# Joined attention runs, reworked reciprocal roots and a rearranged closing norm in a hybrid encoder layer

## The chip, the cores and the metric

The kernel runs on one core of one Trainium2 chip. The metric is the device time of one execution in microseconds; the median of three runs is given. The profile comes from one further execution and has its own time.

## The reference

One layer on 512 tokens of width 2048 (a grid of 8 rows by 64 columns). All arrays are float32.

```python
xn = rms_norm(x, attn_norm_g[l])
proj = jnp.einsum("bsd,dc->bsc", xn, w_in[l])
u_val, u_gate, q, k, v = jnp.split(proj, split_pts, axis=-1)      # 1024 columns each
y_conv = conformer_conv(u_val, u_gate, ...)   # GLU, depthwise conv of 31, layer norm, swish
y_na = neighborhood_attention(heads(q), heads(k), heads(v), rpb[l])   # 16 heads of 64
mixed = jnp.concatenate([rms_norm(y_conv, conv_out_g[l]), rms_norm(y_na, na_out_g[l])], axis=-1)
x = x + jnp.einsum("bsc,cd->bsd", mixed, w_out[l])
xn = rms_norm(x, ffn_norm_g[l])
up = depthwise_conv(jnp.einsum("bsd,df->bsf", xn, w_up[l]), ffn_dw_w[l], ffn_dw_b[l])   # width 3
gate, val = jnp.split(up, 2, axis=-1)                              # 5632 columns each
x = x + jnp.einsum("bsf,fd->bsd", jax.nn.silu(gate) * val, w_down[l])
return rms_norm(x, final_norm_g)
```

The attention lets each token see a window of 8 rows by 16 columns around it, with a learned bias per head and offset, softmax over the 128 positions, and a weighted sum of the values.

## The kernel before

Activations stand transposed: 128 channels on the partitions, 512 tokens along the free axis. Every large matmul is done with split operands: a float32 matrix is written as a high part (what float32r keeps) and a low part (the rest), and three float32r products stand for one float32 product. For a weight unit of 128 x 1024 `parts` (L123) makes the high half on ACT (`whi`, L126) and the low half on VectorE (`wlo`, L127).

The stages, in order of time, are:

1. Input projection, up to about 505 us. `project` (L334) makes one block of 128 columns in two units of eight channel blocks. `group` (L146) issues for each unit 16 matmuls with `whi` (L150, L151) and then eight with `wlo` (L153): 24 matmuls. `ORDER` (L59) fixes which blocks come when: an "a" is a gate and a value block of the convolution group, a "q" is the query, key and value blocks of a pair of heads.
2. Output projection (`out_half`, L566), first the convolution half, then the attention half.
3. The up projection (`up`, L706), in a seven-product (Strassen) form, 44 hidden tiles, with the depthwise convolution of width 3 behind each (`hidden`, L771; its taps on VectorE are L763 and L764).
4. The down projection (`product2`, L837), also of seven products, over the hidden tiles, most of which were written to HBM and come back through `again` (L809).
5. The closing norm (`ready`, `write`).

Small work between the large matmuls is written as generators. `tick` (L158) is called after each unit: it takes the next step of the first generator in `steps` and of the first in `asteps`, and places its instructions after the unit's last matmul. So one step stands on TensorE between two groups of 24 matmuls. Inside that, a scheduler orders each engine's instructions by priority; `shifted` (L85) moves the priority, `pin` keeps instructions in the order in which they were written.

`attend` (L450) is the generator of one pair of heads. Its steps before the change, one per tick:

- the value tile's transposes (`trv`, L458) and the load of the first bias table (L521);
- `scores(0)`: for two of the four blocks of 128 queries, both heads, a matmul of 64 rows on 256 keys (L470) into the one PSUM tile with the tag "sc"; then for each head bias (L478), maximum (L480), exponentials on ACT (L483), reciprocal (L484) and scaling on ACT (L486);
- the second table;
- `scores(2)` and the first `turn`: the transposes (`trp`, L498) of the first two blocks' weights, one PSUM tile with the tag "tr" (two buffers) per head, and ACT's copy of each (L503);
- `values(0)`: the products with the values (L512);
- the second `turn`;
- `values(2)`, the copy and the split.

The convolution taps (L384, 30 for each of eight tiles, on VectorE) run alongside at a later priority, each on the accumulator `y` of its tile.

`root_steps` (L232) makes an inverse root of 512 sums: a root on ACT, a reciprocal and one Newton step on VectorE (L237 to L241), a diagonal matrix per 128 tokens (L245), and one float32 matmul with ones (L248) that spreads the result over all partitions. It is run five times. PSUM for it comes from `stat` (L225), the "sc" tile up to the output projection, "tr" after.

`TURN2` (L55) is the order of the down projection's products. Its operands are made by `operand` (L783): a copy on ACT (L801), a subtraction on VectorE (L802). The first two (`KEEP // 2`) are made ahead, during the last hidden tile, in `again`.

In the last product (`TAIL`, L57) the four banks end one after the other. For each, `ready` (L893) adds the residual (L898) and sums squares on ACT (L900); when both banks of a token block are done `write` (L905) forms the inverse root and scales and stores the rows.

Of the kernel before, what the change touches and what calls it, by code (L numbers as in the profile page):

```python
# [10 lines left out]
F32 = mybir.dt.float32  # L11
F32R = mybir.dt.float32r
AF = mybir.ActivationFunctionType
# [3 lines left out]
P = 128  # L17
# [56 lines left out]
def layer(ctx: ExitStack, tc: tile.TileContext, xT, xn, w_in, w_out, w_up, w_down, par, tab, g3, out):  # L74
# [17 lines left out]
    def t2(name, dt=F32):  # L92
        return tp.tile([P, S], dt, tag="t2k", name=name)
# [20 lines left out]
    eps = consts.tile([P, 1], F32, name="eps")  # L114
    nc.vector.memset(eps, EPS)
    ident = consts.tile([P, P], F32, name="ident")
    make_identity(nc, ident)

# [113 lines left out]
    def root_steps(sums, n, name):  # L232

        v, r, y = (sm.tile([P, S // P], F32, tag="rs" + c, name="rs" + c) for c in "vry")
        nc.vector.tensor_scalar(v, sums, 1.0 / n, EPS, op0=ALU.mult, op1=ALU.add)
        nc.scalar.activation(r, v, AF.Sqrt)
        nc.vector.reciprocal(r, r)  # L237
        nc.vector.tensor_mul(y, v, r)
        nc.vector.tensor_mul(y, y, r)
        nc.vector.tensor_scalar(y, y, -0.5, 1.5, op0=ALU.mult, op1=ALU.add)  # L240
        nc.vector.tensor_mul(y, y, r)  # L241

        dg = t2("dg")
# [4 lines left out]
        nc.tensor.matmul(ps, ones, dg, start=True, stop=True)  # L248
        res = t2(name)
        nc.scalar.activation(res, ps, AF.Copy)  # L250
        return res
# [198 lines left out]
    def attend(p, q, k, v):  # L450


        hps = [slice(j * DH, (j + 1) * DH) for j in range(2)]
        vt = []
        for half in range(2):
            ps = psa.tile([P, 4, P], F32, tag="tr", name="trv", bufs=2)
            for c in range(4):
                nc.tensor.transpose(ps[:, c, :], v[half][:, c // 2, c % 2 * P:(c % 2 + 1) * P], ident)  # L458
            t = t2("vt").rearrange("p (c k) -> p c k", c=4)
            nc.scalar.activation(t, ps, AF.Copy)  # L460
            vt.append(t)
        po = psa.tile([P, S], F32, tag="po", name="po")
        soft = []

        def scores(b0):
            both = psa.tile([P, 2, 2, 2 * P], F32, tag="sc", name="sc")
            for i in range(2):
                b = b0 + i
                for j, hp in enumerate(hps):
                    m = nc.tensor.matmul(both[:, j, i, :], q[hp, b * P:(b + 1) * P], grid(k, KC0[b], KW)[hp],  # L470
                                         start=True, stop=True)
                    if i or j:
                        pin(m)
            two = tabs.pop(0)
            for j in range(2):
                tb = two[:, j]
                s = t2("s").rearrange("p (i k) -> p i k", i=2)
                nc.vector.scalar_tensor_tensor(s, both[:, j], DH ** -0.5, tb, op0=ALU.mult, op1=ALU.add)  # L478
                nm = sm.tile([P, 2], F32, tag="nm", name="nm")
                nc.vector.tensor_reduce(nm, s, axis=AX.X, op=ALU.max, negate=True)  # L480
                su = sm.tile([P, 2], F32, tag="su", name="su")
                for i in range(2):
                    nc.scalar.activation(s[:, i], s[:, i], AF.Exp, bias=nm[:, i:i + 1], accum_out=su[:, i:i + 1])  # L483
                nc.vector.reciprocal(su, su)  # L484
                for i in range(2):
                    nc.scalar.activation(s[:, i], s[:, i], AF.Copy, scale=su[:, i:i + 1])  # L486
                soft.append(s)

        pts = []

        def turn():
            pts.clear()
            for j in range(2):
                s = soft.pop(0)
                ps = psa.tile([P, 4, P], F32, tag="tr", name="trp", bufs=2)
                for i in range(2):
                    for ch in range(2):
                        m = nc.tensor.transpose(ps[:, 2 * i + ch, :], s[:, i, ch * P:(ch + 1) * P], ident)  # L498
                        if i or j or ch:
                            pin(m)  # L500
                pt = t2("pt").rearrange("p (c k) -> p c k", c=4)
                with shifted(-SOONER):
                    nc.scalar.activation(pt, ps, AF.Copy)  # L503
                pts.append(pt)

        def values(b0):
            for i in range(2):
                b = b0 + i
                for ch in range(2):
                    for j in (1, 0):  # L510
                        hp = hps[j]
                        m = nc.tensor.matmul(grid(po, b * BLK, BLK)[hp], vt[b // 2][:, 2 * (b % 2) + ch, hp],  # L512
                                             pts[j][:, 2 * i + ch, :], start=(ch == 0), stop=(ch == 1))
                        if (i, ch, j) != (0, 0, 1):
# [378 lines left out]
    def ready(x, ps, th, dh, only=range(2 * Q), fused=()):  # L893

        for i in only:
            t, d = divmod(i, Q)
            d += Q * dh
            add(x[i], x[i], ps[i])  # L898
            q = t2("sq")
            nc.scalar.activation(q, x[i], AF.Square, accum_out=sq[th][:, t, d:d + 1])  # L900
            if i not in fused:
                nc.vector.tensor_mul(x[i], x[i], gs[d])
            yield

    def write(th, t, ys, fused=()):  # L905
        v, r, y = (sm.tile([P, 1], F32, tag="rs" + c, name="rs" + c) for c in "vry")
        nc.vector.tensor_reduce(v, sq[th][:, t], axis=AX.X, op=ALU.add)
        nc.scalar.activation(r, v, AF.Sqrt, scale=1.0 / D, bias=eps)
        nc.vector.tensor_scalar(v, v, 1.0 / D, EPS, op0=ALU.mult, op1=ALU.add)
        nc.vector.reciprocal(r, r)  # L910
        nc.vector.scalar_tensor_tensor(y, v, r, r, op0=ALU.mult, op1=ALU.mult)
        nc.vector.tensor_scalar(y, y, -0.5, 1.5, op0=ALU.mult, op1=ALU.add)
        nc.vector.tensor_mul(y, y, r)
        for d in reversed(range(Q)):
            for dh in range(2):
                i = t * Q + d
                x = ys[dh][i]
                if dh:
                    nc.scalar.activation(x, x, AF.Copy, scale=y)
                elif i in fused:  # L920
                    nc.vector.scalar_tensor_tensor(x, x, y, gs[d], op0=ALU.mult, op1=ALU.mult)
# [35 lines left out]
    for i in product2(5, a, False):  # L957
        with shifted(-100):
            for _ in ready(e3, a, 0, 0, (i,), fused):
                pass  # L960
        if i % Q == Q - 1:
            for _ in write(0, i // Q, (e3, e0), fused):
                pass


# [60 lines left out]
```

## Time and profile before

| what | us |
|---|---|
| median of 3 runs | 1992.7 (1992.6 to 1993.33) |
| the profiled execution, its time | 1993.17 |
| its span | 1991.4 |
| TensorE busy (PE) | 1976.7 |
| VectorE busy (DVE) | 1593.1 |
| ScalarE busy (ACT) | 1100.4 |
| mean granted TensorE clock | 0.998 |

Engines are PE (matmuls), PEld (weight loads), DVE (VectorE), ACT (ScalarE), POOL (GpSimd) and SP (which issues DMAs). A line such as L470 is a line of the kernel. The page's second part divides the span into 40 slices, each digit the busy share in tenths. The chain of waits is followed back from the last instruction to what released it; its rows give start, length and what. A timeline row gives start, length, engine, line, operation, tile written and read, shape, and in brackets the engine's idle time before it and what ended it. A row of grouped instructions ends in busy time, mean duration in ns, and idle time before. A row of a window gives each engine's busy time and count in the order PE, PEld, DVE, ACT, POOL, then the granted clock, the DMA share and GB/s. Matmuls are pipelined, so the duration of one is longer than the distance to the next.

### The profile page before, as it was taken

Reading aid. Unit: us, or ns where it says so; the run is one execution under the profiler, and the core shown is the slowest. Engines: PE = TensorE matmul, PEld = TensorE weight load, DVE = VectorE, ACT = ScalarE, POOL = GpSimd, SP = SyncE. Lnnn points to the kernel's source line nnn. Section 1 sums busy time; section 2 is a strip of 40 time slices with the busy share of each in tenths; the row PEclk is TensorE's granted clock in tenths of the full one; section 3 lists DMA queues with packets and bytes.
Section 4 is the critical chain, followed back from the end, with each engine's and each line's share of the span. In section 5 each row is a group of like instructions: output and inputs, shape, how many; then the busy total and the mean of one; then the engine's idle time right before and its main releaser. Section 6 shows DMA issues by size and latency. Waiting matters only on the chain.

```text
span 1991.4 us, 28519 instructions
## 1 busy us (share of the span) xinstructions
PE 1976.7 (99%) x10525; PEld 1685.7 (85%) x10525; DVE 1593.1 (80%) x2296; ACT 1100.4 (55%) x1728; POOL 225.4 (11%) x310
## 2 busy tenths in 40 slices
PE   9999999999999999999999999999999999999998
PEld 7878888887788888989898898989898888888886
DVE  5995798498547888888888888888888898886764
ACT  7244423438525675666666666656666644554653
POOL 0111111110001111111111111111110400000000
PEclk9999999999999999999999999999999999999999
DMA  9676667666857889999999999999986967666563
GB/s 345 176 219 186 170 169 209 182 181 186 278 148 199 216 220 271 243 267 247 262 252 257 263 245 262 248 265 244 268 228 179 362 244 231 220 215 195 192 201 116
DMA packets 143117, 451.04 MB, mean 226 GB/s; under 512 B 15232, under 2 KB 23936, under 8 KB 141568
## 3 DMA queue, kind: packets, MB, share of 16 engines
q1 hardware_dynamic: 90608, 293.98, 43.2%
q0 software_dynamic: 42624, 148.92, 34.8%
q10 hardware_dynamic: 9744, 6.30, 1.0%
q8 instruction: 83, 1.36, 0.3%
q14 instruction: 58, 0.48, 0.1%
HBM read 430.27 MB, written 111.15 MB: 272 GB/s over the span
## 4 chain that ended last, share of the span: by engine, by line
PE 96%; DVE 2%; DMA 1%; ACT 0%; issue 0%; SPq 0%; DVEq 0%
PE pu L720 37%; PE pd L848 21%; PE pj L150 7%; PE pj L153 7%; PE pj L151 7%; PE po L150 3%; PE po L151 3%; PE po L153 3%; PE pu L143 2%; PE pu L142 2%; PE pu L139 2%; DVE y L384 1%; PE sc L470 1%; PE po L512 1%; PE trp L498 1%; DMA raw<-in_w_in 0%
## 5 line engine op out<-in xcount | busy, mean ns | idle before, releaser
L127 DVE TENSOR_TENSOR wlo<-raw,whi 128x1024 fp32r<-128x1024 f32 x572 | 694.6, 1222 | 285.2 <-ACT whi L126 221.4
L126 ACT ACTIVATE whi<-raw 128x1024 fp32r<-128x1024 f32 x572 | 600.7, 1058 | 572.7 <-PE pj L151 168.0
L720 PE MATMUL pu<-xc,whi 128*128 128x512 f32 x2112 | 505.5, 391 | 0.1
L720 PEld LDWEIGHTS pu<-xc,whi 128*128 128x128 f32 x2112 | 388.0, 188 | 75.3 <-DVE xc L603 0.3
L848 PE MATMUL pd<-whi,ho 128*128 128x512 f32 x1232 | 305.1, 389 | 1.4 <-DVE vl L733 1.4
L720 PEld LDWEIGHTS pu<-xc,wlo 128*128 128x128 f32 x2112 | 274.4, 191 | 10.3
L720 PE MATMUL pu<-xc,wlo 128*128 128x256 f32 x2112 | 282.3, 283 | 0.0
L848 PEld LDWEIGHTS pd<-whi,ho 128*128 128x128 f32 x1232 | 231.0, 188 | 50.3 <-DVE vl L733 1.8
L150 PE MATMUL pj<-xh,whi 128*128 128x512 f32 x608 | 241.4, 397 | 0.0
L151 PE MATMUL pj<-xl,whi 128*128 128x512 f32 x608 | 237.6, 391 | 0.0
L384 DVE SCALAR_TENSOR_TENSOR y<-ch,prm,y 128x510 f32<-128x510 f32 (+14 forms) x240 | 169.8, 739 | 3.1
L848 PE MATMUL pd<-wlo,ho 128*128 128x512 f32 x616 | 165.0, 389 | 0.0
L153 PE MATMUL pj<-xh,wlo 128*128 128x512 f32 x608 | 150.4, 389 | 0.8 <-DVE wlo L127 0.8
L729 ACT ACTIVATE pu<-pu 128x512 f32<-128x512 f32 x132 | 76.5, 580 | 121.4 <-PE pu L720 121.2
L150 PEld LDWEIGHTS pj<-xh,whi 128*128 128x128 f32 x608 | 114.2, 188 | 27.4 <-issue 4.9
L848 PEld LDWEIGHTS pd<-wlo,ho 128*128 128x128 f32 x616 | 115.6, 188 | 24.0
L153 PEld LDWEIGHTS pj<-xh,wlo 128*128 128x128 f32 x608 | 114.0, 188 | 24.9 <-DVE wlo L127 1.2
L151 PEld LDWEIGHTS pj<-xl,whi 128*128 128x128 f32 x608 | 114.2, 188 | 23.5 <-issue 1.1
L205 POOL DMA_DIRECT2D ws<-in_w_down x88 | 79.5, 904 | 363.8 <-DMA ws<-in_w_down 132.9
L664 POOL DMA_DIRECT2D raw<-in_w_up x88 | 78.0, 887 | 286.3 <-DVE wlo L127 114.5
L139 PE MATMUL pu<-xc,whi 128*128 128x256 f32 x352 | 99.6, 283 | 0.0
L142 PE MATMUL pu<-xc,whi 128*128 128x256 f32 x352 | 99.6, 283 | 0.0
(189 smaller groups left out, 2322.9 us busy)
## 6 DMA issues: line engine op xcount, KB each, us to landing
raw<-in_w_up SPq DMA_DIRECT2D x220, 512.0 KB, 5.5
ws<-in_w_down POOLq DMA_DIRECT2D x132, 512.0 KB, 6.3
raw<-in_w_up POOLq DMA_DIRECT2D x88, 512.0 KB, 8.6
raw<-ws SPq DMA_DIRECT2D x88, 512.0 KB, 3.5
raw<-in_w_in SPq DMA_DIRECT2D x78, 512.0 KB, 5.1
raw<-in_w_down SPq DMA_DIRECT2D x66, 512.0 KB, 3.7
ws<-ws POOLq DMA_DIRECT2D x44, 512.0 KB, 5.5
raw<-in_w_out SPq DMA_DIRECT2D x32, 512.0 KB, 5.4
```

The costliest lines, as they stand in the source:

```text
L126: i = nc.scalar.activation(hi[:, :n], raw[:, :n], AF.Copy)
L127: j = nc.vector.tensor_sub(lo[:, :n], raw[:, :n], hi[:, :n].bitcast(F32))
L139: i = nc.tensor.matmul(ps, hi[:, a], mh, start=start, stop=False, skip_group_check=more)
L142: nc.tensor.matmul(ps, hi[:, a], ml, start=False, stop=False, skip_group_check=more)
L150: nc.tensor.matmul(ps, hi, mh, start=first and k == 0, stop=False)
L151: nc.tensor.matmul(ps, hi, ml, start=False, stop=False)
L153: i = nc.tensor.matmul(ps, lo[:, wk * P:(wk + 1) * P], mh, start=False, stop=last and k == len(ws) - 1)
L205: nc.gpsimd.dma_start(wsum[c][k], w_down[k, {1: A21, 2: A11, 4: A11, 6: A12}[c]], accum_op=ALU.add, max_dma_last_dim=ROW)
L384: nc.vector.scalar_tensor_tensor(y[:, a:b], h[:, a + j - PAD:b + j - PAD], prm[:, o + j:o + j + 1], y[:, a:b], op0=ALU.mult, op1=ALU.add)
L664: nc.gpsimd.dma_start(a[c], w_up[f, q2], accum_op=ALU.add)
L720: i = nc.tensor.matmul(ps[:, :n], part[:, k * P:(k + 1) * P], comb[c][k][:, :n], start=j == 0 and not more, stop=j == 2 * U - 1, skip_grou ...
L848: m = nc.tensor.matmul(ps[i], h[:, o + t * P:o + (t + 1) * P], w[:, d], start=start and not more and kind == 0 and j == 0, stop=stop and k ...
```

## The change

Five edits:

- `attend`: `scores(0)` and `scores(2)` are issued in one run of eight matmuls, the first half into "sc", the second into the two "tr" tiles, then both softmaxes; both tables are loaded in the first step. The first `turn` puts both heads into one "sc" tile, the second into two "tr" tiles, each in a step of its own; `values(0)` and `values(2)` make one run of sixteen. The generator has five steps instead of seven.
- `root_steps`: 2 r / (v + r²) with r the root takes the place of reciprocal and Newton step. The result is split into a high and a low part, each with its own diagonal, and two float32r matmuls spread it.
- `write`: the same formula; all but the last sum of squares are summed beforehand (`all_but_one`), and the last enters the root as ACT's scaled input with the rest as bias.
- `ready`: the sums' columns are ordered so that the last one to be formed is the last column.
- `again`: a third operand is made ahead, at the fourth product of the last hidden tile.

```diff
-    ones = consts.tile([P, P], F32, name="ones")
+    ones_r = consts.tile([P, P], F32R, name="ones")
+    ones = ones_r.bitcast(F32)
...
+        h = sm.tile([P, S // P], F32R, tag="rsh", name="rsh")
         nc.vector.tensor_scalar(v, sums, 1.0 / n, EPS, op0=ALU.mult, op1=ALU.add)
         nc.scalar.activation(r, v, AF.Sqrt)
-        nc.vector.reciprocal(r, r)
-        nc.vector.tensor_mul(y, v, r)
-        nc.vector.tensor_mul(y, y, r)
-        nc.vector.tensor_scalar(y, y, -0.5, 1.5, op0=ALU.mult, op1=ALU.add)
-        nc.vector.tensor_mul(y, y, r)
-
-        dg = t2("dg")
-        for i in range(S // P):
-            nc.vector.tensor_scalar(dg[:, i * P:(i + 1) * P], ident, y[:, i:i + 1], None, op0=ALU.mult)
+        nc.vector.tensor_mul(y, r, r)
+        nc.vector.tensor_add(y, y, v)
+        nc.vector.reciprocal(y, y)
+        nc.vector.scalar_tensor_tensor(y, y, 2.0, r, op0=ALU.mult, op1=ALU.mult)
+        nc.vector.tensor_copy(h, y)
+        nc.vector.tensor_sub(v, y, h.bitcast(F32))
+
+        dg = [t2("dg", F32R) for _ in range(2)]
+        for d, x in zip(dg, (h.bitcast(F32), v)):
+            for i in range(S // P):
+                nc.vector.tensor_scalar(d[:, i * P:(i + 1) * P], ident, x[:, i:i + 1], None, op0=ALU.mult)
         yield
         ps = stat()
-        nc.tensor.matmul(ps, ones, dg, start=True, stop=True)
+        for i in range(2):
+            nc.tensor.matmul(ps, ones_r, dg[i], start=i == 0, stop=i == 1)
...
-        def scores(b0):
-            both = psa.tile([P, 2, 2, 2 * P], F32, tag="sc", name="sc")
+        def scores(b0, both, more=False):
...
-                    if i or j:
+                    if more or i or j:
                         pin(m)
+
+        def softmax(both):
             two = tabs.pop(0)
...
-        def turn():
-            pts.clear()
+        def turn(two, more=False):
             for j in range(2):
-                s = soft.pop(0)
-                ps = psa.tile([P, 4, P], F32, tag="tr", name="trp", bufs=2)
+                s, ps = soft.pop(0), two[j]
...
         table(0)
-        yield
-        scores(0)
-        yield
         table(2)
         yield
-        scores(2)
-        turn()
+        both = psa.tile([P, 2, 2, 2 * P], F32, tag="sc", name="sc")
+        both = [both[:, j] for j in range(2)]
+        more = [psa.tile([P, 2, 2 * P], F32, tag="tr", name="sc", bufs=2) for _ in range(2)]
+        scores(0, both)
+        scores(2, more, True)
+        softmax(both)
+        softmax(more)
+        yield
+        both = psa.tile([P, 2, 4, P], F32, tag="sc", name="trp")
+        turn([both[:, j] for j in range(2)])
+        yield
+        turn([psa.tile([P, 4, P], F32, tag="tr", name="trp", bufs=2) for _ in range(2)])
         yield
         values(0)
-        yield
-        turn()
-        yield
-        values(2)
+        values(2, True)
...
-        if at == 1:
-            pre.extend(operand(TURN2[0], k) for k in order2[:KEEP // 2])
+        if at in (1, 3):
+            pre.extend(operand(TURN2[0], k) for k in order2[len(pre):KEEP // 2 + (at > 1)])
...
+    def all_but_one(th, t):
+
+        m = sm.tile([P, 1], F32, tag="nm", name="rsm")
+        nc.vector.tensor_reduce(m, sq[th][:, t, :2 * Q - 1], axis=AX.X, op=ALU.add)
+        nc.vector.tensor_scalar(m, m, 1.0 / D, EPS, op0=ALU.mult, op1=ALU.add)
+        return m
+
+    def write(th, t, ys, most=None, fused=()):
+        most = most or all_but_one(th, t)
         v, r, y = (sm.tile([P, 1], F32, tag="rs" + c, name="rs" + c) for c in "vry")
-        nc.vector.tensor_reduce(v, sq[th][:, t], axis=AX.X, op=ALU.add)
-        nc.scalar.activation(r, v, AF.Sqrt, scale=1.0 / D, bias=eps)
-        nc.vector.tensor_scalar(v, v, 1.0 / D, EPS, op0=ALU.mult, op1=ALU.add)
-        nc.vector.reciprocal(r, r)
-        nc.vector.scalar_tensor_tensor(y, v, r, r, op0=ALU.mult, op1=ALU.mult)
-        nc.vector.tensor_scalar(y, y, -0.5, 1.5, op0=ALU.mult, op1=ALU.add)
-        nc.vector.tensor_mul(y, y, r)
+        last = sq[th][:, t, 2 * Q - 1:]
+        nc.scalar.activation(r, last, AF.Sqrt, scale=1.0 / D, bias=most)
+        nc.vector.tensor_scalar(v, last, 1.0 / D, most, op0=ALU.mult, op1=ALU.add)
+        nc.vector.scalar_tensor_tensor(v, r, r, v, op0=ALU.mult, op1=ALU.add)
+        nc.vector.reciprocal(v, v)
+        nc.vector.tensor_scalar(y, v, r, 2.0, op0=ALU.mult, op1=ALU.mult)
...
+            if i % Q == Q - 2:
+                most = all_but_one(0, i // Q)
```

More of the change, by code (lines that the diff above doesn't have):

```diff
@@ L113, in layer @@
         nc.tensor.matmul(ps[:, :P], ones, ones, start=True, stop=True)
-    eps = consts.tile([P, 1], F32, name="eps")
-    nc.vector.memset(eps, EPS)
     ident = consts.tile([P, P], F32, name="ident")
@@ L469, in scores @@
                 for j, hp in enumerate(hps):
-                    m = nc.tensor.matmul(both[:, j, i, :], q[hp, b * P:(b + 1) * P], grid(k, KC0[b], KW)[hp],
+                    m = nc.tensor.matmul(both[j][:, i, :], q[hp, b * P:(b + 1) * P], grid(k, KC0[b], KW)[hp],
                                          start=True, stop=True)
-                    if i or j:
+                    if more or i or j:
                         pin(m)
+        def softmax(both):
             two = tabs.pop(0)
@@ L477, in scores @@
                 s = t2("s").rearrange("p (i k) -> p i k", i=2)
-                nc.vector.scalar_tensor_tensor(s, both[:, j], DH ** -0.5, tb, op0=ALU.mult, op1=ALU.add)
+                nc.vector.scalar_tensor_tensor(s, both[j], DH ** -0.5, tb, op0=ALU.mult, op1=ALU.add)
                 nm = sm.tile([P, 2], F32, tag="nm", name="nm")
@@ L498, in turn @@
                         m = nc.tensor.transpose(ps[:, 2 * i + ch, :], s[:, i, ch * P:(ch + 1) * P], ident)
-                        if i or j or ch:
+                        if more or i or j or ch:
                             pin(m)
@@ L504, in turn, with values @@
                 pts.append(pt)
-        def values(b0):
+        def values(b0, more=False):
             for i in range(2):
@@ L512, in values @@
                         m = nc.tensor.matmul(grid(po, b * BLK, BLK)[hp], vt[b // 2][:, 2 * (b % 2) + ch, hp],
-                                             pts[j][:, 2 * i + ch, :], start=(ch == 0), stop=(ch == 1))
-                        if (i, ch, j) != (0, 0, 1):
+                                             pts[b0 + j][:, 2 * i + ch, :], start=(ch == 0), stop=(ch == 1))
+                        if more or (i, ch, j) != (0, 0, 1):
                             pin(m)
@@ L896, in ready @@
             t, d = divmod(i, Q)
+            o = d + Q * (1 - dh)
             d += Q * dh
@@ L899, in ready @@
             q = t2("sq")
-            nc.scalar.activation(q, x[i], AF.Square, accum_out=sq[th][:, t, d:d + 1])
+            nc.scalar.activation(q, x[i], AF.Square, accum_out=sq[th][:, t, o:o + 1])
             if i not in fused:
@@ L960, in layer @@
                 pass
+            if i % Q == Q - 2:
+                most = all_but_one(0, i // Q)
         if i % Q == Q - 1:
-            for _ in write(0, i // Q, (e3, e0), fused):
+            for _ in write(0, i // Q, (e3, e0), most, fused):
                 pass
```

1 line of the change is left out of this document (removed).

## The prediction

> **What bounds the kernel now.** I read the page first, then the chain of waits.
>
> ```profile
> span 1991.4 us, 28519 instructions
> PE 1976.7 (99%) x10525; PEld 1685.7 (85%) x10525; DVE 1593.1 (80%) x2296; ACT 1100.4 (55%) x1728; POOL 225.4 (11%) x310
> ...
> DVE  5995798498547888888888888888888898886764
> ...
> PE 96%; DVE 2%; DMA 1%; ACT 0%; issue 0%; SPq 0%; DVEq 0%
> ```
>
> TensorE carries the chain almost everywhere, so each edit is worth what it takes from or adds to TensorE's stream. The exception is the slices where VectorE is at 9 (50 to 150 us): there the chain leaves TensorE. The chain in order of time (start, length, what) gives the prices of small runs:
>
> ```profile
> 107.48 1.81 PE pj L153 x8
> 112.92 1.82 PE pj L153 x8
> ...
> 119.25 1.81 PE pj L153 x8
> 121.06 1.06 PE sc L470 x8
> ...
> 125.98 1.81 PE pj L153 x8
> ...
> 133.23 1.06 PE sc L470 x8
> ...
> 138.99 1.81 PE pj L153 x8
> 140.80 1.02 PE po L512 x16
> ...
> 145.68 1.82 PE pj L153 x8
> ...
> 152.01 1.81 PE pj L153 x8
> ...
> 574.11 0.86 PE st L248 x2
> ```
>
> A group of 24 projection matmuls ends each 5.44 us (107.48 to 112.92), 0.227 each. From the end of one group (121.06) to the end of the next (125.98 + 1.81 = 127.79) with a scores run between is 6.73: the run costs 1.29. Likewise a values run costs 147.50 - 140.80 - 5.44 = 1.26, transposes alone 153.82 - 147.50 - 5.44 = 0.88, scores with transposes behind them 140.80 - 133.23 - 5.44 = 2.13. A root's matmul costs 0.86.
>
> **Runs joined.** Timeline rows of single instants show the spacing inside runs:
>
> ```profile
> 121.31 0.38 PE L470 MATMUL sc<-k,q 64*128 64x256 f32 x2
> 121.53 0.38 PE L470 MATMUL sc<-k,q 64*128 64x256 f32 x2
> 141.00 0.49 PE L512 MATMUL po<-pt,vt 128*64 128x128 f32 x5
> 141.11 0.49 PE L512 MATMUL po<-pt,vt 128*64 128x128 f32 x5
> ```
>
> Scores go in pairs every 0.215 us, four pairs a run: 0.86 is work and 0.43 of the 1.29 is entering and leaving. Values go in pairs every 0.11, eight a run: 0.39 of 1.26 is fixed. Joining saves each fixed part once per head pair. It could be nothing, if a longer run pays inside what it saves outside, and no more than the two fixed parts; the even spacing speaks for all of it: 8 x 0.82 = 6.6. Setting the transposes apart from the scores loses 1.29 + 0.88 - 2.13 = 0.04 each, 0.3 in all. **Gain 6.3.**
>
> **Roots.** One f32 matmul of 0.86 becomes two split ones. No row shows them with these operands; between nothing gained and two projection matmuls (0.45) I take the latter, same shape and type: 0.41 each. The first of five precedes a VectorE wait (next part) and only lengthens it: **gain 4 x 0.41 = 1.6.** The added VectorE operations (one small, four diagonal) lie beside projections, which need only the row sums' result a group later; uncovered they would cost about 1.0 per root (five at 0.2).
>
> **Tables.** The second table of a pair is now loaded with the first, one step sooner, ahead of weights on SP's queue and one slot of the nine weight buffers longer.
>
> ```profile
> raw<-in_w_in SPq DMA_DIRECT2D x78, 512.0 KB, 5.1
> ```
>
> A load of the same size lands in 5.1 us; weights are made three units, so three groups of 5.44, ahead: **0**. Without that lead each table would cost up to 5.1.
>
> **What VectorE does to the joined runs.** The changed program's order of instructions, with these rows, is where time is lost:
>
> ```profile
> 98.52 2.03 DVE L384 SCALAR_TENSOR_TENSOR y<-ch,prm,y 128x505 f32<-128x505 f32 x3
> 100.47 2.35 DVE L127 TENSOR_TENSOR wlo<-raw,whi 128x1024 fp32r<-128x1024 f32 x2
> 101.74 1.43 PE L153 MATMUL pj<-xh,wlo 128*128 128x512 f32 x5 [0.81 <-DVE wlo L127]
> 120.67 2.31 DVE L384 SCALAR_TENSOR_TENSOR y<-ch,prm,y 128x508 f32<-128x508 f32 x3
> 124.70 1.28 DVE L478 SCALAR_TENSOR_TENSOR s<-sc,tab 128x512 f32<-128x512 f32 x2
> 120.99 1.13 PE L470 MATMUL sc<-k,q 64*128 64x256 f32 x8
> 129.32 0.91 ACT L486 ACTIVATE s<-s,su 128x256 f32<-128x256 f32 x2 [1.12 <-DVE su L484]
> ```
>
> TensorE already waits 0.81 for the low weight halves (wlo). In the changed order five convolution taps instead of three stand between the key copy and these two wlo; two taps at 0.65 (alternating accumulators) push wlo and TensorE by **1.3**. Everything on TensorE follows.
>
> Then the first head pair. Before, scores end at 122.12, VectorE starts the softmax at 124.70, 2.6 late because of taps, and ACT has head 0's weights scaled at 130.23, 5.5 later: 8.1 from the scores. The transposes came two groups (some 12 us) after, so nobody waited. Now they come after one. From the first half's end, TensorE does the second half (0.86), leaves the run (0.1) and does one group (5.44): it arrives after 6.4. VectorE in the new order has two taps more between that wlo and the softmax (at 0.78, as in 2.31 for three on one accumulator) and four others no longer alternate (4 x 0.12): 2.6 + 1.6 + 0.5 = 4.7 late, so ready at 4.7 + 5.5 = 10.2. TensorE waits **3.8**. Below, the wait is nothing if VectorE is not behind (5.5 is under 6.4); above, it is all of 10.2 less 5.4, so 4.8. I take 3.8. Queued behind are all projections; copies and splits on the other engines wait with them, later, with slack.
>
> **Head 1.** Before, each head's transposes had a tile of their own. Now the first turn puts both into the one "sc" tile, and head 1's first transpose carries a wait on ACT; in the order it stands four or five projection matmuls (0.9 to 1.1 us) after head 0's. It waits for ACT's copy of head 0, and ACT has the second half's softmax in its queue:
>
> ```profile
> L503 ACT ACTIVATE pt<-trp 128x512 f32<-128x512 f32 x32 | 17.4, 594 | 24.2 <-PE trp L498 24.2
> L483 ACT ACTIVATE s<-s,nm 128x256 f32<-128x256 f32 x64 | 31.8, 498 | 29.4 <-DVE nm L480 29.4
> L486 ACT ACTIVATE s<-s,su 128x256 f32<-128x256 f32 x64 | 28.6, 496 | 4.4 <-DVE su L484 4.4
> ```
>
> With ACT idle the copy (0.59) is done before TensorE arrives: 0. With four of these 0.5 us operations ahead: 0.59 + 2.0 - 0.9 = 1.7. Pairs whose softmax is late also wait at head 0, and the last pair's scores, which now need both "tr" tiles, wait for their value copies. I take 0.7 per pair, between the ends, nearer the idle one because ACT is 55% busy: 8 x 0.7 = **5.6.**
>
> **Third operand.**
>
> ```profile
> 1565.33 1.20 PE L848 MATMUL pd<-whi,ho 128*128 128x512 f32 x4 [1.41 <-DVE vl L733]
> 1570.90 2.21 PE L848 MATMUL pd<-whi,ho 128*128 128x512 f32 x8
> 1571.45 0.75 DVE L802 TENSOR_TENSOR ho<-h,ho 128x256 fp32r<-128x256 f32 x2
> ```
>
> The down projection stalls 1.41 for its third operand, which the change makes earlier by one copy on ACT and one subtraction on VectorE, both moved ahead of the last hidden tile's folds. But the next operands (L802 at 1571.45) stand on VectorE behind the last hidden tile's four taps, and TensorE meets them with no room (eight matmuls take 2.21, not 8 x 0.227 = 1.8 and a tail). Arriving 1.4 earlier it waits there instead. Between 0 and 1.4 gained, I take **0.1**.
>
> **End.**
>
> ```profile
> 1983.93 0.18 ACT L900 ACTIVATION_READ_ACCUMULATOR sq<-xr 128x1 f32 x1
> 1984.34 0.29 ACT L908 ACTIVATE rsr<-rsv,eps 128x1 f32<-128x1 f32 x1 [0.23 <-DVE rsv L907]
> 1984.93 0.22 DVE L911 SCALAR_TENSOR_TENSOR rsy<-rsv,rsr 128x1 f32<-128x1 f32 x1
> 1985.57 0.75 DVE L921 SCALAR_TENSOR_TENSOR xr<-xr,rsy,g 128x512 f32<-128x512 f32 x1
> ```
>
> From the last sum (1984.11) to its first use (1985.57) is 1.46. After: the root at once on ACT (0.29 and two handovers, 0.08), then three small VectorE steps as from 1984.93 to 1985.57 (0.64): 1.0. **Gain 0.5**, between 0 and 0.9 (if one of the three were free).
>
> **Sum.** Gains 6.3 + 1.6 + 0.1 + 0.5 = 8.5; losses 1.3 + 3.8 + 5.6 = 10.7: 2.2 slower. The profiled execution took 1993.2 with a span of 1991.4, 0.5 over the median of 1992.7; added to the profiled time 1995.4, to the median 1994.9. I take 1995.4, on the high side for the clock below.
>
> **Rivals.** (a) The change does what it is written to do and no wait comes: 6.3 + 5 x 0.41 + 1.4 + 0.5 = 10.3, 1982.4. For it speaks that ACT and VectorE are not full over the stage; against it that at 124.70 VectorE was 2.6 late, and one group is shorter than 8.1. 7%. (b) Only the first pair waits: 8.5 - 1.3 - 3.8 = 3.4 faster, 1989.3. For it the idle-ACT end of head 1's bound. 13%. (c) Slower: head 1 waits the 1.7 of a full ACT queue in every pair: 13.6 for 5.6, 2003. It decides from 0.95 per pair on, where the total passes 1996.7. Against it ACT's 55%. 11%. (d) The clock falls in the gap.
>
> ```profile
> 1981.13 1.07 PE L848 MATMUL pd<-wlo,ho 128*128 128x512 f32 x4
> 1983.00:1985.00 2.00, 0.00 (x0) 0.00 (x0) 0.81 (x5) 1.02 (x3) 0.00 (x0) 0.85 1.02 376
> 1985.00:1987.00 2.00, 0.00 (x0) 0.00 (x0) 1.61 (x5) 1.33 (x2) 0.00 (x0) 0.50 0.23 82
> ```
>
> TensorE's work ends at 1982.2; the granted clock averages 0.85 over the next window but one and is 0.50 after, so it halved about 2.2 us into idleness (at 0.85, 0.6 of the 2 us were at half). A 3.8 us gap at the first pair is longer. If half speed then lasts as long as the gap, 1.9 are lost: 1997.3. No row shows it last. 21%. The Trainium skill, "TensorE: Matmul & The Clock Gate", section "What's actually happening", puts both the idle window that halves the clock and the busy one that restores it at about 3.4 us. The trace agrees that idleness halves it, but after less. By that page the loss would be an estimated 1.7.
>
> **How the numbers follow.** My forecast, 1995.4, has 48%; its own range is 1992.5 to 1998. Three runs lie within 0.04%; 0.2%, 4.0 us, is about what a measurement of this kernel can tell from no change, so the bounds are 1988.7 and 1996.7. Faster: all of (a) and a third of (b), 0.11. Slower: about three tenths of the forecast, two thirds of (d), nearly all of (c), 0.39. Same: 0.50. The range 1988.5 to 2000.5 takes in most of (b) and the nearer part of (c).
>
> **What would show it.** Right: 16 scores records in one run costing about 2.15 instead of 2.58; a TensorE wait of 3 to 5 us at the first transposes; waits of 0.5 to 1 on ACT's copy before head 1's; wlo's wait near 101 us above 2; a down-projection stall of 1.4 at the fourth operand; 1.0 from last sum to first use. Wrong: transposes that wait nowhere, or value products that find their transposes' copies late as well, which I cost at nothing because a whole group (5.44) stands between them.

## The result and the profile after

The changed kernel takes 1998.01 us (median of 9 runs, 1997.78 to 1999.25) against 1992.7 before (9 runs, 1992.44 to 1993.33): a ratio of 1.0028, 95% interval 1.002 to 1.0037. It is slower, by 5.3 us, 2.6 more than forecast. Of the ten executions of `x_operands2` below, one took 2165.76 at a mean granted clock of 0.85, where the other nine had 0.997 or more, and its median is that of the nine. The profiled execution took 1997.95; its page, beside that of before:

```profile
span 1996.0 us, 28535 instructions
PE 1975.9 (99%) x10525; PEld 1690.3 (85%) x10525; DVE 1596.8 (80%) x2320; ACT 1099.4 (55%) x1728; POOL 225.4 (11%) x310
...
PE 90%; DVE 6%; ACT 2%; issue 1%; DMA 1%; SPq 0%; DVEq 0%
```

TensorE has as many instructions as before and is as busy; VectorE has 24 more. What changed is the chain of waits: TensorE's share of it fell from 96% to 90%, VectorE's rose from 2% to 6%. The time is lost in waits, and the timeline of TensorE shows where they begin (start, length, what, and in brackets the idle time ahead of it and who ended it):

```profile
102.26 3.52 PE L152 MATMUL pj<-xh,wlo 128*128 128x512 f32 x8 [2.48 <-DVE wlo L126]
...
123.16 2.00 PE L472 MATMUL sc<-k,q 64*128 64x256 f32 x16
...
132.76 0.99 PE L500 MATMUL trp<-ident,s 128*128 128x128 f32 x4 [1.90 <-ACT s L490]
135.26 1.05 PE L500 MATMUL trp<-ident,s 128*128 128x128 f32 x4
```

TensorE's wait for the low weight halves (wlo) near 101 us is 1.67 longer than before (2.48 of idleness for 0.81), the joined scores are one run of 2.00, and the first head pair's transposes, which waited for nobody before, wait 1.90 for the softmax. Eight matmuls on wlo last 3.52 at 102.26; the same eight take about 2 elsewhere. The reason stands in the busy time by stretches (span of the stretch, its length, busy time and instructions on TensorE, its weight loads, VectorE, ScalarE, GpSimd; then the granted clock). The stretches are cut at 3.413 us, where the clock changes:

```profile
99.18:102.60 3.42, 0.94 (x5) 0.47 (x3) 3.42 (x5) 0.31 (x1) 0.00 (x0) 1.00 0.10 18
102.60:106.01 3.41, 3.41 (x10) 2.67 (x9) 3.41 (x5) 0.75 (x1) 0.00 (x0) 0.50 0.72 232
106.01:109.42 3.41, 3.41 (x16) 2.82 (x15) 3.41 (x5) 0.00 (x0) 0.51 (x1) 1.00 1.05 375
...
129.90:133.32 3.42, 1.52 (x8) 0.82 (x7) 3.42 (x8) 2.38 (x9) 0.51 (x1) 1.00 0.83 256
133.32:136.73 3.41, 3.41 (x12) 2.78 (x12) 3.31 (x7) 2.92 (x10) 0.00 (x0) 0.50 0.56 217
```

Twice a stretch with a wait in it is followed by one stretch of exactly 3.413 us at half clock, called a halving from here on. The kernel before had none until its last matmul. At half clock 3.41 us do the work of 1.7.

The other waits, from TensorE's groups of instructions by shape (busy and mean length, then the idle time ahead of the whole group and who ended it):

```profile
L500 PE MATMUL trp<-ident,s 128*128 128x128 f32 x128 | 20.6, 283 | 4.4 <-ACT s L490 2.7 <-ACT pt L505 1.6
L472 PE MATMUL sc<-k,q 64*128 64x256 f32 x128 | 16.0, 389 | 0.8 <-ACT ra L253 0.8
```

TensorE waits 4.4 us over all transposes, 1.6 of it behind copies of the other head (pt), and 0.8 before the last pair's scores, behind ScalarE's copy of a root (ra); before the change, both groups waited for nothing. TensorE's timeline in the down projection:

```profile
1576.77 1.20 PE L854 MATMUL pd<-whi,ho 128*128 128x512 f32 x4 [1.28 <-DVE ho L808]
```

The stall is still there, one operand further on. And the timeline of all engines in the closing norm:

```profile
1988.59 0.19 ACT L907 ACTIVATION_READ_ACCUMULATOR sq<-xr 128x1 f32 x1
...
1989.13 0.22 DVE L925 SCALAR_TENSOR_TENSOR rsv<-rsr,rsv 128x1 f32<-128x1 f32 x1
...
1989.84 0.75 DVE L935 SCALAR_TENSOR_TENSOR xr<-xr,rsy,g 128x512 f32<-128x512 f32 x1
```

From the last sum (1988.78) to its first use (1989.84) it now takes 1.06, where it took 1.46.

### The profile page after: what moved, and what is told of

Read it like the earlier page. It is cut to its first block, busy times and chain, and to the rows that moved or that the text cites. A ratio compares the mean times of both kernels' runs of the same rounds, so it can differ in the third digit from the quotient of the medians.

```text
span 1996.0 us, 28535 instructions
## 1 busy us (share of the span) xinstructions
PE 1975.9 (99%) x10525; PEld 1690.3 (85%) x10525; DVE 1596.8 (80%) x2320; ACT 1099.4 (55%) x1728; POOL 225.4 (11%) x310
## 4 chain that ended last, share of the span: by engine, by line
PE 90%; DVE 6%; ACT 2%; issue 1%; DMA 1%; SPq 0%; DVEq 0%
PE pu L726 37%; PE pd L854 20%; PE pj L152 5%; PE pj L149 5%; PE pj L150 5%; PE po L152 3%; PE po L149 3%; PE po L150 3%; DVE y L387 3%; PE pu L141 2%; PE pu L142 2%; PE pu L138 2%; DVE wlo L126 1%; PE po L514 1%; PE trp L500 1%
## 5 line engine op out<-in xcount | busy, mean ns | idle before, releaser
L726 PE MATMUL pu<-xc,whi 128*128 128x512 f32 x2112 | 505.6, 391 | 0.1
L726 PE MATMUL pu<-xc,wlo 128*128 128x256 f32 x2112 | 282.3, 283 | 0.0
L387 DVE SCALAR_TENSOR_TENSOR y<-ch,prm,y 128x505 f32<-128x505 f32 (+14 forms) x240 | 169.9, 740 | 3.1
L142 PE MATMUL pu<-xc,wlo 128*128 128x256 f32 x352 | 99.7, 283 | 0.0
L141 PE MATMUL pu<-xc,whi 128*128 128x256 f32 x352 | 99.7, 283 | 0.0
```

Source lines behind the costliest of these rows:

```text
L141: nc.tensor.matmul(ps, hi[:, a], ml, start=False, stop=False, skip_group_check=more)
L142: return nc.tensor.matmul(ps, lo[:, a], mh, start=False, stop=stop, skip_group_check=more)
L387: nc.vector.scalar_tensor_tensor(y[:, a:b], h[:, a + j - PAD:b + j - PAD], prm[:, o + j:o + j + 1], y[:, a:b], op0=ALU.mult, op1=ALU.add)
L726: i = nc.tensor.matmul(ps[:, :n], part[:, k * P:(k + 1) * P], comb[c][k][:, :n], start=j == 0 and not more, stop=j == 2 * U - 1, skip_grou ...
```

## The experiments

Two theories were set against each other. Theory W: waits that the new order makes on TensorE (and the clock that falls behind them) eat what the joined runs and roots save. Rivals: the joined runs save nothing in themselves (J), or the attention is a gain and the loss comes from the rest (R). The kernel before ran again beside each group of experiments, with medians of 1992.6 to 1993.0, so a difference between kernels of different groups is good to about 0.4.

### The two halves of the change

`x_attend_only` is the kernel before with the new attention pair and nothing else; `x_no_attend` is the changed kernel with the old one.

```diff
-        scores(0)
-        yield
...
-        scores(2)
-        turn()
+        scores(0, both)
+        scores(2, more, True)
+        softmax(both)
+        softmax(more)
         yield
...
+        turn([both[:, j] for j in range(2)])
         yield
+        turn([psa.tile([P, 4, P], F32, tag="tr", name="trp", bufs=2) for _ in range(2)])
+        yield
+        values(0)
+        values(2, True)
```

> The kernel before with the new attend alone; old roots, old end, two operands ahead. Theory W (the joined runs bring their own waits: head 0's transposes come before the softmax is done, head 1's wait for ACT's copy of head 0): the 6.3 us that joining saves are more than used up, 1994 to 1996.5, with a gap of about 2 us before the first transposes and no longer wait for wlo than before (1 us or less at 101 us). Theory R (the loss comes from the roots' added VectorE work, the attention edit gains): 1986 to 1988, no gap before the first transposes.

> The changed kernel with the old attend; new roots, new end, third operand. Theory W: roots 4 x 0.4 and the end 0.5 gained, less 1.3 to 1.7 for the later wlo (its wait at 101 us stays 2.5) and up to 1.7 if the clock halves there: 1991 to 1993. Theory R: as slow as the changed kernel, 1997 to 1999.

Measured: the attention alone 1996.26 (ratio 1.0017, 1.0008 to 1.0027); the rest alone 1993.35 (1.0001, 0.9992 to 1.0011), just above what was expected. R is out: the attention pair by itself costs 3.5. Its first transposes wait 1.57 for head 0 and 0.41 for head 1, together the 2 that were expected, and its wlo waits the old 0.81. All its transposes, by shape:

```profile
L497 PE MATMUL trp<-ident,s 128*128 128x128 f32 x128 | 20.4, 278 | 4.6 <-ACT s L487 2.5 <-ACT pt L502 2.1
```

The waits at the transposes come with the attention alone, and no clock was lost in this execution. The rest alone shows the other half. Its busy time by stretches:

```profile
99.20:102.62 3.42, 1.21 (x6) 0.67 (x4) 3.42 (x5) 0.00 (x0) 0.00 (x0) 1.00 0.39 71
102.62:106.03 3.41, 3.14 (x7) 2.48 (x8) 3.41 (x5) 1.06 (x1) 0.00 (x0) 0.50 0.55 161
```

So the late wlo and the first halving come without the new attention. The two halves alone add up to 4.2, the change costs 5.3. The second halving, at 133.32, comes only where both are present; that it makes up the 1.1 is likely, but was not measured by itself.

### The first root

`x_first_root` is the changed kernel with the old root for the first norm only; the other roots stay new.

```diff
-        rstd.append((yield from root_steps(sums, D, "rstd1")))
+        rstd.append((yield from old_root_steps(sums, D, "rstd1")))
```

> The changed kernel with the old form of the first root alone (the statistics of the first norm); the second root is new. Theory W: in the new order VectorE has more to do before the two rounded wlo tiles, the wait for wlo near 100 us (2.5 in the changed kernel, 0.97 before) goes back to about 1.0, the clock is not halved at 102.6, TensorE comes to the first transposes earlier and so waits longer there (3 to 4 instead of 1.9); the sum is 1993.5 to 1995.5. Rival: wlo is late for another reason (the third operand made early, or the order of the other chunks): the wait stays at 2.4 and the time at 1997 to 1998.

Measured: 1993.92 (1.0006, 0.9997 to 1.0015), 4.1 less than the changed kernel. Two waits from its timeline of TensorE:

```profile
101.40 0.96 PE L152 MATMUL pj<-xh,wlo 128*128 128x512 f32 x3 [0.81 <-DVE wlo L126]
...
129.96 0.84 PE L521 MATMUL trp<-ident,s 128*128 128x128 f32 x4 [1.56 <-ACT s L511]
```

the first operation of the softmax on its VectorE:

```profile
124.37 1.28 DVE L503 SCALAR_TENSOR_TENSOR s<-sc,tab 128x512 f32<-128x512 f32 x2
```

and the same operation of the changed kernel:

```profile
127.18 1.28 DVE L482 SCALAR_TENSOR_TENSOR s<-sc,tab 128x512 f32<-128x512 f32 x2
```

The wait for wlo is back at 0.81 and the clock stays whole, as W said, and the rival (a wait that stays at 2.4) is out. One number of W's expectation missed: the transposes wait 1.56, not 3 to 4. The softmax says why. It starts at 124.37, against 127.18 in the changed kernel, and the transposes start 5.6 behind it in both (129.96, 132.76). VectorE sets that time, and the new form of the first root makes it 2.8 later: five more operations of its own on VectorE, and behind them another order of taps and wlo.

### The tile that two heads share, and the step between

`x_tr` gives the first turn the two "tr" tiles instead of halves of one "sc" tile; `x_step` keeps the shared tile and puts one more step (a group of projections) between scores and first turn; `x_step_tr` does both.

```diff
         softmax(more)
         yield
+        yield
-        both = psa.tile([P, 2, 4, P], F32, tag="sc", name="trp")
-        turn([both[:, j] for j in range(2)])
+        turn([psa.tile([P, 4, P], F32, tag="tr", name="trp", bufs=2) for _ in range(2)])
```

> The changed kernel with the first turn's two heads in two tiles (tag tr) instead of one tile (tag sc); all else the same. Theory W: head 1's transposes no longer wait for ACT's copy of head 0, about 0.3 us a pair less, 1995 to 1996.5; the gap before the first pair's transposes stays. Rival S (head 1 waits for its own softmax): no change, 1998.

> The changed kernel with one more step between a pair's scores and its first turn, and the shared tile for both heads' transposes kept. Theory W: the extra work covers the first head's softmax, but the second head's transposes still wait for ScalarE's copy of the first, .3 to .8 in each pair and more in the first: 1993 to 1996. Rival: the step alone is enough, as in the version with two tiles: 1990.7.

> As x_tr, and one more step (one more group of projection matmuls) between the scores and the first turn. Theory W: hardly any wait at transposes is left, so the 6.3 of the joined runs are seen: 1986.5 to 1990 (the later wlo and one halving of the clock remain). Rival J (joined runs save nothing, the length of the run is what costs): 1993 or more.

| kernel | median us | ratio, 95% interval |
|---|---|---|
| tiles alone (`x_tr`) | 1996.55 | 1.0019, 1.001 to 1.0029 |
| step alone (`x_step`) | 1996.45 | 1.0017, 1.0008 to 1.0027 |
| both (`x_step_tr`) | 1990.73 | 0.9987, 0.9978 to 0.9997 |

Each alone gives 1.5 back; both give 7.3. All three lie above what was expected, the first by 0.05, the second by 0.45 and the third by 0.7; the third because the joined runs save less than the 6.3 put down for them, as a later part shows. TensorE's wait at the first pair, tiles alone:

```profile
132.34 1.97 PE L500 MATMUL trp<-ident,s 128*128 128x128 f32 x8 [3.48 <-ACT s L490]
```

step alone, the wait and then the group:

```profile
142.36 1.12 PE L500 MATMUL trp<-ident,s 128*128 128x128 f32 x4 [3.84 <-ACT pt L505]
```

```profile
L500 PE MATMUL trp<-ident,s 128*128 128x128 f32 x128 | 19.4, 280 | 5.1 <-ACT pt L505 4.8 <-ACT s L490 0.3
```

and the group with both:

```profile
L500 PE MATMUL trp<-ident,s 128*128 128x128 f32 x128 | 18.0, 274 | 0.3 <-ACT s L490 0.3
```

With tiles alone head 0 waits for its softmax (s). With the step alone head 0 is in time, and head 1 stands 3.84 behind ScalarE's copy of head 0 (pt): what the step takes away at one place comes back at the next. Only both together leave 0.3. This also decides against J: `x_step_tr` differs from `x_no_attend` (1993.35) in the joined attention alone, both have the late wlo, and the joined form is 2.6 faster. The step alone was profiled in its slowest execution of ten (1999.59), which lost two stretches of clock behind the 3.84 and one near 15 us; what the faster ones lost is in no trace.

### The operands of the down projection

`x_operands` makes six operands ahead instead of three.

```diff
-        if at in (1, 3):
-            pre.extend(operand(TURN2[0], k) for k in order2[len(pre):KEEP // 2 + (at > 1)])
+        if at in (1, 3, 4):
+            pre.extend(operand(TURN2[0], k) for k in order2[len(pre):{1: 2, 3: 3, 4: 6}[at]])
```

By the third call the first operand has been taken from `pre`, so `len(pre)` is two: the third operand is made twice, and four products of the first pass use a neighbour's. `x_operands2` counts the operands by themselves (`order2[slice(*{1: (0, 2), 3: (2, 3), 4: (3, 6)}[at])]`).

> The changed kernel with six down-projection operands made ahead (2, 3 and 6 at the three places). If the stall in the down-projection belongs to the first operand that is made behind the last gate, six ahead leave time enough: no wait over 0.3 on VectorE's operands, 1.1 to 1.4 us less, 1996 to 1997. Rival: the stall only moves on to the next operand, as it did from the third to the fourth: 1998.

> The changed kernel with six down-projection operands made ahead, each once and each for its own product (in x_operands the third was made twice, and the products from the third on took their neighbour's operand). If the stall belongs to the first operand made behind the last gate: no wait over .3 in the down-projection, 1.1 to 1.6 less than the changed kernel, 1996 to 1997. Rival: the operand that was made twice is what removed it, and the stall comes back: 1998.

Measured: 1996.47 and 1996.92, both within the 1996 to 1997 expected. In both the stall is gone. The down projection of `x_operands2` by shape, which waited 1.4 before and 1.3 in the changed kernel:

```profile
L854 PE MATMUL pd<-whi,ho 128*128 128x512 f32 x1232 | 305.1, 389 | 0.0
```

and two waits from its timeline, to which a later part returns:

```profile
102.44 0.73 PE L152 MATMUL pj<-xh,wlo 128*128 128x512 f32 x2 [2.48 <-DVE wlo L126]
...
132.94 1.12 PE L500 MATMUL trp<-ident,s 128*128 128x128 f32 x4 [3.51 <-ACT s L490]
```

The stall belongs to the first operand behind the last gate; one operand more made ahead hands it on, three further ones end it. The gain in the medians is 1.1 to 1.5 against a stall of 1.3, and `x_operands2` shows that it does not come from the operand that `x_operands` makes twice.

### All together

`x_best` and `x_best2` have the step, the two tiles, the old first root and six operands ahead; `x_best` with the operands as in `x_operands` (the same products take a neighbour's operand), `x_best2` with them as in `x_operands2`.

> One more step before the first turn, two tiles for the transposes, the old first root and six operands ahead, together. If the savings add up: no wait over 1.0 at wlo, none over .5 at the transposes, none in the down-projection, the clock never halved before the last matmul: 1984.5 (1983.5 to 1986), faster than both kernels. Rival: the waits are taken out but their time comes back elsewhere (savings not additive): 1988 or more.

> x_best with the six operands mended in the same way, so that it computes the reference: one more step, two tiles for the first turn, the old first root. Expected as x_best: 1985.4 to 1986.8, faster than both kernels. Rival: the mended operands bring a wait back: 1988.

Measured: 1986.42 and 1985.84 (ratio 0.9967, 0.9954 to 0.9979): 6.8 less than before and 12.2 less than the changed kernel. `x_best` missed the edge of what was expected by 0.4; its rival (1988 or more) is out. The waits of `x_best2`:

```profile
L521 PE MATMUL trp<-ident,s 128*128 128x128 f32 x128 | 18.0, 275 | 0.3 <-ACT s L511 0.3
...
L493 PE MATMUL sc<-k,q 64*128 64x256 f32 x128 | 16.0, 389 | 0.8 <-ACT ra L274 0.8
```

Beside these, wlo's old 0.81 is the only wait of TensorE over 0.2 that is left between 30 us and its last matmul.

### The clock by itself

`x_stalls_short` and `x_stalls_long` hold TensorE up in the up projection of `x_best2`, where it otherwise waits for nobody: 14 times by one ScalarE copy, or 4 times by five. The long form is shown; the short one has `range(4, 32, 2)` and `range(1)`.

```diff
+                    if j == 0 and held:
+                        behind(i, held)
+            if f in range(4, 32, 7) and c == 4:
+                z = t2("gap")
+                for j in range(5):
+                    held = nc.scalar.activation(z, comb[3][0].bitcast(F32), AF.Copy)
+                    if j == 0:
+                        behind(held, i)
+                gap.append(held)
```

> x_best2 with TensorE held up 14 times, once in each of 14 up-projection chunks, by one ScalarE copy of 128x512 (.63 in the trace) that starts when a product ends and that the next product waits for. Theory (a window of 3.4 with up to 1.4 of idle time in it keeps its clock): each costs its own idle time and nothing else, .8 to 1.1 each, 11 to 15 over x_best2, and the clock is not halved there. Rival (any wait of this kind loses clock): 1.7 more each, over 30.

> x_best2 with TensorE held up 4 times by five ScalarE copies each (5 x .63 and the way to ScalarE and back: 3.3 to 3.6 idle). Theory (1.9 of idle time within one window of 3.413 halves the clock for the next window): 13.2 to 14.4 of idle time and 3 or 4 halvings of 3.413 at 1.7 each, 18.5 to 21 over x_best2. Rival (only a window that is idle from end to end loses the clock): 13 to 15 over x_best2 and no halving; or the idle time costs less because other work catches up in it.

Measured: 2006.55 and 2013.04, which is 20.7 and 27.2 over `x_best2`. The held matmuls by shape, short and then long:

```profile
L750 PE MATMUL pu<-xc,whi 128*128 128x512 f32 x2112 | 509.8, 392 | 16.9 <-ACT gap L759 16.9
```

```profile
L750 PE MATMUL pu<-xc,whi 128*128 128x512 f32 x2112 | 512.5, 394 | 18.7 <-ACT gap L759 18.6
```

and the long one by stretches, from the first of its stalls:

```profile
780.14:783.55 3.41, 1.59 (x7) 0.95 (x6) 3.41 (x5) 2.36 (x6) 0.00 (x0) 1.00 0.96 233
783.55:786.96 3.41, 0.58 (x3) 0.49 (x4) 1.44 (x2) 2.72 (x4) 0.50 (x1) 1.00 1.02 376
786.96:790.38 3.42, 3.42 (x12) 2.85 (x11) 0.00 (x0) 0.65 (x1) 0.36 (x1) 0.50 0.99 247
```

With 1.8 more of idle time the four long stalls cost 6.5 more than the fourteen short ones. A short stall has 1.21 of idle time (16.9 / 14) and costs 1.48 (20.7 / 14). The clock is whole, so the other 0.27 is put down to its ends, where matmuls no longer overlap: the group's busy time is 4.2 longer than in `x_best2` (505.6), 0.30 a stall. A long one has 4.7, costs 6.8, and is followed by one stretch at half clock, four times of four: 6.8 - 4.7 - 0.27 leaves 1.8 for it, where 3.413 at half speed makes 1.7. Both totals lie 6 above what was expected (11 to 15 and 18.5 to 21), for two reasons. The idle times are longer: the short ones 1.21 instead of 0.8 to 1.1, the long ones 4.7 instead of 3.3 to 3.6, where ScalarE's queue put a weight copy (1.04) between the copies that hold TensorE up. And the ends, which the expectation put at nothing, add 3.8 to the fourteen and 1.1 to the four. The rival that any wait costs clock (over 30 for the short ones) is out. The rival of a window idle from end to end is out: in the row at 783.55 TensorE was busy for 0.58.

## Why the prediction was right and where it was wrong

The time lies in the range, the sign of the sum was right, and its size was half of what came (2.7 against 5.3 over the median). By the prediction's own bounds 1998.01 is slower (above 1996.7), a case that it gave 0.39, less than the 0.50 for no change; the nearest of its cases is rival (d), 1997.3. Point by point:

- **The attention pair.** The sum had -6.3 for the joined runs, +3.8 for the first transposes and +5.6 for head 1: 3.1. `x_attend_only` has a span of 1994.8 against 1991.4, so 3.4. The agreement is luck: the saving and the waits were both put too large, and the errors cancel. What a pair saves can be read where nothing waits, between the same matmuls of before

```profile
206.13 0.39 PE L150 MATMUL pj<-xh,whi 128*128 128x512 f32 x1
...
262.79 0.39 PE L150 MATMUL pj<-xh,whi 128*128 128x512 f32 x1
...
580.29 0.39 PE L150 MATMUL po<-mah,whi 128*128 128x512 f32 x1
...
714.45 0.61 PE L720 MATMUL pu<-xc,whi 128*128 128x512 f32 x2
```

  and after

```profile
211.56 0.39 PE L149 MATMUL pj<-xh,whi 128*128 128x512 f32 x1
...
267.61 0.39 PE L149 MATMUL pj<-xh,whi 128*128 128x512 f32 x1
...
585.56 0.39 PE L149 MATMUL po<-mah,whi 128*128 128x512 f32 x1
...
719.30 0.62 PE L726 MATMUL pu<-xc,whi 128*128 128x512 f32 x2
```

  the distance of the first two is 56.66 and 56.05: 0.61, not 0.79, so 4.9 for eight pairs. Against it stands idle time of 4.6 at the transposes and 0.8 at the last scores in nine waits; with 0.27 for the ends of each, as the short stalls have it, 7.8, for 9.4 in the sum. 7.8 - 4.9 is 2.9 of the 3.4; the last 0.5 is not accounted for.
- **Head 1.** The sum had one wait of 0.7 in each of eight pairs, 5.6. The changed kernel has four waits of 0.17 to 0.67 behind ScalarE's copies, 1.6 together, and about as much again before the scores and transposes of the last two pairs (4.4 + 0.8 - 1.90 = 3.3 in all). The cause was right; the sum had too many and too long waits.
- **The first transposes.** The forecast was a wait of 3.8. It is 3.51 in `x_operands2` and 3.48 in `x_tr`, which share the late wlo and kept whole clock at it. With the old first root it is 1.57 (`x_attend_only`), so VectorE's lateness, as forecast, makes most of it. It is 1.90 in the changed kernel's profiled execution only because TensorE, slowed at 102.6, came later to a softmax whose time VectorE sets (the transposes start at 132.76, and at 132.94 in `x_operands2`). That first halving therefore cost next to nothing.
- **The step that failed is the clock.** The sum had no term for it, only a choice between two totals on the high side, worth 0.5; rival (d) had one halving, at the first transposes, at 21%. That one came, at 133.32, and lost 1.7, where 1.9 had been put. The error was to hold it for a rival when the forecast itself had a wait of 3.8 there and the quoted row put the halving 2.2 into idleness. For wlo the prediction saw only the wait (1.3 later, and 0.41 longer by the first root: 1.7, measured 1.67) and not that 2.48 of idleness is enough for a halving of its own. The Trainium skill, "TensorE: Matmul & The Clock Gate", section "What's actually happening", has the clock fall after at least one idle window, about 3.4 us. The length of the window agrees (3.413), the condition doesn't: 1.90 idle within one window did it here.
- **The first root** was booked as lengthening the wlo wait by its own 0.41, at no cost. It costs 4.1 (1998.01 less 1993.92): VectorE's added operations make the softmax 2.8 later, and the clock falls. Costing them at nothing "beside projections" was right for TensorE's next group and wrong for VectorE's queue, which was full there (3.42 of 3.42 in the row at 99.18). The second norm's root gained what was put down: across it, the distance of the last two matmuls in the same fences went from 134.16 to 133.74, 0.42. The other three were not measured one by one.
- **The third operand** went as written: the stall (1.41) moved to the fourth (1.28), gain about nothing.
- **The end** gave 0.40 between last sum and first use, where 0.5 was forecast.
- **Rival (a)**, no waits at all, 1982.4, is what `x_best2` tries to reach; 1985.84 is what it came to, with joined runs at 0.61 instead of 0.79 a pair, one old root and 1.1 of waits left.
- **Rival (c)** passes 1996.7 from 0.86 per pair on, counted from the 1995.4 that was forecast (1.3 / 8 over 0.7), not from 0.95.

## What to carry to other kernels

A saving on a full engine counts only if the engines that feed it are as early as before: look first at which of them sets the time of the next consumer, since time lost or won ahead of that point only changes the length of the wait. When a wait has two causes in a row (a late softmax, then a shared buffer), taking away either alone brings little; take away both before judging the idea. And price a gap on TensorE twice, once for its length and once for the clock: one of 1.4 us costs little more than itself, one of 2 to 2.5 may cost 1.7 more, depending on where it falls.

## What the runs showed of the hardware

The granted clock works in stretches of 3.413 us on a fixed grid: in the changed kernel the two halvings lie 30.72 apart, nine times 3.413, and the four in `x_stalls_long` 143.36, forty-two times. Over the fourteen executions profiled, from 30 us to the last matmul, each stretch in which TensorE was idle for 1.90 or more was followed by one at half clock, and none at whole clock with up to 1.82 was (the row at 780.14 has 3.41 - 1.59 = 1.82 and whole clock behind it; the row at 129.90 has 1.90 and half clock). So the same wait can cost 1.7 or nothing. In the changed kernel the 2.48 before wlo lies in one stretch; in `x_operands2` the grid cuts it in two:

```profile
97.82:101.23 3.41, 2.14 (x10) 1.45 (x8) 3.41 (x7) 0.00 (x0) 0.00 (x0) 1.00 0.66 119
101.23:104.65 3.42, 2.21 (x10) 1.83 (x11) 3.42 (x5) 1.06 (x1) 0.00 (x0) 1.00 0.30 64
```

1.27 and 1.21 idle, and no halving. The grid stands elsewhere in each execution, and the spread of the runs seems to follow it (one execution of each kernel has a trace): `x_step_tr`, which has this one wait, ran at 1990.5 to 1990.9 with a mean clock of 0.998 and twice at 1988.7 and 1989.4 with 0.999.

Twice, in `x_step` and in `x_operands2`, the half clock lasted for two stretches though TensorE was busy for 2.4 of the first. The one of `x_operands2`:

```profile
131.95:135.37 3.42, 2.43 (x8) 2.02 (x9) 3.35 (x8) 2.99 (x9) 0.90 (x1) 0.50 0.78 295
135.37:138.78 3.41, 3.41 (x11) 2.73 (x10) 2.90 (x7) 2.80 (x10) 0.00 (x0) 0.50 0.83 115
```

and the stretch behind the wait in `x_tr`, which whole clock followed:

```profile
131.65:135.06 3.41, 2.72 (x11) 2.26 (x12) 3.34 (x8) 3.28 (x9) 0.00 (x0) 0.50 0.49 169
```

In the two cases TensorE was idle for 0.98 and 1.00 of the stretch at half clock; in the thirteen others it was idle for 0.69 at most, and whole clock followed each. So at half clock less idle time seems to be enough to keep the clock low than at whole clock; with two cases, where the limit lies is open. Where a joined pair loses the 0.18 between 0.79 and 0.61 was not tried.
